# Evacuation priority, spread values, a third bank and the order of table functions in a hybrid decoder step

## The chip, the cores and the metric

The kernel runs on one core of one Trainium2 chip. Its time is the device time of one execution in microseconds. A core has five engines with a queue each: TensorE (matmuls and the loads of their stationary operand), VectorE, ScalarE, GpSimd and SyncE, which here issues the DMAs. Each queue is worked off in the order in which it was written. TensorE writes to PSUM, eight banks of 512 float32 values per partition, and VectorE or ScalarE must read ("evacuate") a bank before it can be used again; GpSimd has no part in that.

## The reference

One step of a one-layer decoder for a prompt of 512 tokens and 8 sample sequences of 4 tokens each, 544 columns in all, with a model width of 1024:

```python
h  = RMSNorm_pre(x)
P  = h @ w_in      # GLU value | gate | r | k | v | low-rank decay, iclr, gate | merge gates
A  = GLU -> causal depthwise conv (31) -> LayerNorm -> swish -> projection
# RWKV-7, per head of 64:
decay = exp(-exp(w_log));  a = sigmoid(iclr_base + l_iclr @ w_iclr_up)
kk = k * k_k;  kk = kk * rsqrt(max(sum(kk * kk), 1e-24))
s  = s * w_t - (s @ kk) (kk * a) + v k      # per token
y  = s @ r
B  = ((group_norm(y) + bonus) * g) -> projection
x  = x + RMSNorm_post((sigmoid(gA) * A + sigmoid(gB) * B) @ w_out)
x  = x + RMSNorm_post2(relu(RMSNorm_pre2(x) @ w_ff_up)^2 @ w_ff_down)
```

Outputs are both groups' tokens and the new states of the convolution, the token shift and the recurrence.

## The kernel before, in words

Channels lie on partitions and tokens on columns. A product with weights is made in three matmuls: each float32 operand is split into an upper and a lower part, and upper x upper, upper x lower and lower x upper are summed in one bank. `part_steps` (L145) writes such a product for one half of the columns (272 or 276 of them): 8 blocks of the contraction, 24 matmuls, then a call of `evac`, which is given by the caller and reads the bank. Weights arrive by DMA (`wraw`), are split by `wsplit` into an upper part (a cast on ScalarE or, for most blocks of `w_in`, on GpSimd, L140) and a lower part (VectorE, L141).

There are three stages. The first normalises the input (to about 50 us). The second (to about 780 us) works through eight pairs of heads and, between them, through the blocks of `w_in`, the gates and the convolution. The third makes the output projections and the feed-forward part and is nearly all linear products.

In the second stage one pair p has these parts. Blocks K, R and W (`block`, L799) are the linear products for k, r and v, with a token-shift evacuation on ScalarE and VectorE (L378 to L386). `rates` (L443) makes the decay and the iclr by two small products with sigmoid evacuations, a running sum of the decay (L460), exponentials of that sum with three different outputs (`pin`, `epp`, `eps`), and the norm of the keys: square, a sum over each head by a matmul (`sum_steps`, L439), a logarithm and an exponential. `front` builds the matrices of the eight chunks of 64 tokens and calls `inverse`, a triangular inverse on VectorE and by matmuls (L608). `value` makes the bonus term. `tokens` transposes. `chain` (L653) is the recurrence over the eight chunks: in each, matmuls into `ch`, a copy to `xs` on ScalarE (L667), a matmul (L671), a scaling on ScalarE (L673), a matmul (L675) and another scaling (L679), each waiting for the one before. `sample` (L692) does the 8 short sequences: it solves for `uv` (L745), spreads it over the sequences into `ux` by eight multiplications with columns of a mask on GpSimd (L754), and multiplies (L758) to update the states `st` (L760, L762). `groupnorm` (L766) follows a pair's recurrence; its last product is evacuated at L795.

The program is written in the order chain(p-1), K, rates, front, R, W, value, tokens, inverse, sample for pair p, then groupnorm(p-1), then `fill`: blocks of linear products for the gates and the convolution, which depend on no pair. This is not the order of the queues. A planner gives each instruction a priority by its place in the program, the earlier the higher, and builds the order of each queue from what is ready by its own cost estimates; `tc.high_priority(offset=n)` moves what is written in it ahead by n places (or back, where n is negative: the convolution runs at -300). The `yield` statements have no effect on that order where a generator is simply run to its end (`run`), or only mark where `until` stops. An engine takes its queue strictly in the planned order.

Three other things set the order. First, `tact` (L232) chains all activations that need a table set in the order of the program, and puts in a load of the set where it changes; `rates` goes through the sets for sigmoid, exponential, logarithm and exponential again, `groupnorm` needs one more. Second, tiles of one tag share the buffers of the tag in turn. Third, PSUM in the second stage: pool `pl` for linear products has 2 banks, `pb` takes 2, and the tags `ax`, `aux`, `yt` and `ch` have one bank each, 8 in all. `ax` serves the rates, all sums over heads, the bonus and the group norm; `aux` the sample part; `yt` and `ch` the recurrence (`ch` also the transposes).

Of the kernel before, what the change touches and what calls it, by code (L numbers as in the profile page):

```python
# [8 lines left out]
F32 = mybir.dt.float32  # L9
# [8 lines left out]
NB = 8  # L18
TS = 4
# [3 lines left out]
C = 64  # L23
# [5 lines left out]
CDEC = math.exp(-0.5)  # L29
NFP, NFIRST, NPG, UB = 44, 6, 2, 2  # L30
KEPT = 2
CP, HP, HN = 300, 900, 130
PUMP, WB, WL, WR = 5, 2, 2, 2
PE, ACT, DVE, SP, POOL = (getattr(mybir.EngineType, e) for e in ("PE", "Activation", "DVE", "SP", "Pool"))

# [27 lines left out]
def hybrid_step(ctx: ExitStack, tc: tile.TileContext, xT, hist, s0, win, wco, wro, wo, wup, wdn, lora,  # L63
# [12 lines left out]
    pg = ctx.enter_context(tc.tile_pool(name="pg", bufs=16))  # L76
    cv = ctx.enter_context(tc.tile_pool(name="cv", bufs=1))
    wp = ctx.enter_context(tc.tile_pool(name="wp", bufs=WB))
    pl = ctx.enter_context(tc.tile_pool(name="pl", bufs=2, space=PSUM))
    dr = ctx.enter_context(tc.tile_pool(name="dr", bufs=1, space=bass.MemoryType.DRAM))  # L80

    vt = cp.tile([128, NV], F32, name="vt")
# [31 lines left out]
    def con(name):  # L114
        o = COFF[name]
        return cs[:, o:o + dict(CONSTS)[name]]
# [28 lines left out]
    def part_steps(w, xs, s, o, m, evac, pool, tag):  # L145

        n = len(w)
        ps = pool.tile([128, 512], F32, name=tag, tag=tag)[:, 0:m]
        for k in range(n):
            (whi, wlo), (xhi, xlo) = w[k], xs[k]  # L150
            for i, (a, b) in enumerate(((whi, xhi), (whi, xlo), (wlo, xhi))):
                nc.tensor.matmul(ps, a, b[:, o:o + m], start=k == 0 and i == 0, stop=k == n - 1 and i == 2)  # L152
            if k == n - 1:
                evac(s, ps, o, m)
            yield

    def part_mm(*args):
# [74 lines left out]
    def tact(name, *args, **kw):  # L232

        with tables(name):
            lastact[0] = act(*args, **kw)
        return lastact[0]
# [42 lines left out]
    def sv(t):  # L279

        return t[:, T:N2].rearrange("p (b t) -> p b t", t=TS)
# [52 lines left out]
    with ExitStack() as c1:  # L334
# [101 lines left out]
        def sum_steps(lhsT, x, evac, pool, tag):  # L436
            for s, (o, m) in enumerate(S2):
                ps = pool.tile([128, 512], F32, name=tag, tag=tag)[:, 0:m]
                nc.tensor.matmul(ps, lhsT, x[:, o:o + m], start=True, stop=True)  # L439
                evac(s, ps, o, m)  # L440
                yield ACT

        def rates(p):  # L443

            lraw = page("k2")[:, 0:128]
            nc.sync.dma_start(lraw, lora[p, :, 0:128])
            yield (ACT,)
            glu_sig()
            yield
            for i in range(2):  # L450
                split_hl(up[0][H[i], i, :], up[1][H[i], i, :], lraw[H[i]])
            yield
            ap_ = p1.tile([128, 2 * N2], F32, name="ap", tag="ap")
            sg, a, pin = page("sg"), ap_[:, 0:N2], ap_[:, N2:2 * N2]
            for i, (d, b) in enumerate(((sg, "decay_base"), (a, "iclr_base"))):
                for s, (o, m) in enumerate(S2):
                    yield from part_steps([(up[0][:, i], up[1][:, i])], [ld], s, o, m,
                                          lambda s, ps, o, m: tact(SIG, d[:, o:o + m], ps, AF.Sigmoid, bias=vec(b, p)),
                                          qc, "ax")
            nc.vector.tensor_tensor_scan(sg[:, 0:N2], con("scan"), sg[:, 0:N2], 0.0, MULT, ADD)  # L460
            ep = p1.tile([128, NC * (C + 1) + 40], F32, name="ep")
            e0 = NC * (C + 1)
            epp = ep[:, 0:e0].rearrange("p (c t) -> p c t", c=NC)
            eps = ep[:, e0:e0 + 40].rearrange("p (b f) -> p b f", f=TS + 1)
            nc.vector.memset(epp[:, :, 0:1], 1.0)
            nc.vector.memset(eps[:, :, 0:1], 1.0)
            yield ACT
            tact(EXP, pin[:, 0:N2], sg[:, 0:N2], AF.Exp, scale=CDEC)
            yield (ACT,)
            tact(EXP, epp[:, :, 1:C + 1], ch3(sg), AF.Exp, scale=-CDEC)  # L470
            yield (ACT,)
            tact(EXP, eps[:, :, 1:TS + 1], sv(sg), AF.Exp, scale=-CDEC)
            yield ("K", p, ACT)

            k = pgs["k", p]
            k2 = page("k2")
            act(k2[:, 0:N2], k[:, 0:N2], AF.Square, scale=vec("k_k", p))
            yield
            rs = page("rs")
            yield from sum_steps(con("blk1"), k2, lambda s, ps, o, m: act(rs[:, o:o + m], ps, AF.Relu, bias=kk_neg), qc, "ax")  # L480
            tact(LN, rs[:, 0:N2], rs[:, 0:N2], AF.Ln, scale=2.0 ** 20, bias=kk_eps)
            yield (ACT,)
            kp = page("k2")
            act(kp[:, 0:N2], a[:, 0:N2], AF.Identity, scale=vec("k_a", p), bias=oka[:, p:p + 1])
            tact(EXP, rs[:, 0:N2], rs[:, 0:N2], AF.Exp, scale=-0.5, bias=kk_log)
            yield DVE
            st2(kp[:, 0:N2], k[:, 0:N2], kp[:, 0:N2], MULT)
            st2(a[:, 0:N2], a[:, 0:N2], pin[:, 0:N2], MULT)
            yield (DVE,)
            kk = page("kk")  # L490
            stt(out=kk[:, 0:N2], in0=k[:, 0:N2], scalar=vec("k_k", p), in1=rs[:, 0:N2], op0=MULT, op1=MULT)
            yield DVE
            pgs["pre"] = ep, epp, eps, a, pin, kk, kp
# [66 lines left out]
        def value(p):  # L560

            f, v, rk = fs[p], pgs["v", p], pgs["k", p]
            bon = f["bon"] = p2.tile([128, N2], F32, name="bon")
            yield from sum_steps(con("blk1"), rk, lambda s, ps, o, m: tt(out=bon[:, o:o + m], in0=ps,
                                                                       in1=v[:, 64 + o:64 + o + m], op=MULT),
                                 qc, "ax")
            if p:
                yield ("smp", p - 1, ACT)
            nc.scalar.copy(vpad[:, :, 32:64], v[:, 64 + T:64 + N2].unsqueeze(1).to_broadcast([128, 2, 32]))
            yield  # L570
# [121 lines left out]
        def sample(p):  # L692
# [55 lines left out]
            for i in range(2):  # L748
                tt(out=y[H[i], :], in0=xy[0:64, 320 + 32 * i:352 + 32 * i],
                   in1=xc[0:64, 64 * i + 32:64 * i + 64], op=ADD)  # L750
            for b in range(0, NB, 4):
                ux = p1.tile([128, 4, 64], F32, name="ux")
                for e in range(4):
                    nc.gpsimd.tensor_scalar(ux[:, e, :], uv[:, 0:64], con("bmask")[:, b + e:b + e + 1], None, MULT)  # L754
                yield
                if b == 0:
                    ps = qc.tile([128, NB, 64], F32, name="aux", tag="aux")
                nc.tensor.matmul(ps[:, b:b + 4].rearrange("p b v -> p (b v)"), zbt, ux.rearrange("p b v -> p (b v)"),  # L758
                                 start=True, stop=True)
            tt(out=st, in0=ps, in1=st, op=ADD)  # L760
            for b in range(NB):
                nc.gpsimd.tensor_scalar(st[:, b, :], st[:, b, :], f["epS"][:, b:b + 1], None, MULT)  # L762
# [3 lines left out]
        def groupnorm(p):  # L766
            f, y = fs[p], pgs["y", p]
            nc.scalar.copy(y[:, T:N2], ys[p])
            yc, sq = page("t0", cv), page("t1", cv)
            lraw = yc[:, 0:128]  # L770
            nc.sync.dma_start(lraw, lora[p, :, 128:256])
            lhi = p1.tile([128, 128], F32R, name="lhi")
            llo = p1.tile([128, 128], F32R, name="llo")
            yield ACT
            split_hl(lhi, llo, lraw)
            yield

            def cevac(s, ps, o, m):
                act(sq[:, o:o + m], ps, AF.Square)
                nc.scalar.copy(yc[:, o:o + m], ps)  # L780
            yield from sum_steps(con("cent"), y, cevac, qc, "ax")
            yield
            rs = sq
            yield from sum_steps(con("blkm"), sq,
                                 lambda s, ps, o, m: tact(LNEXP, rs[:, o:o + m], ps, AF.Ln, bias=gn_eps), qc, "ax")
            tact(LNEXP, rs[:, 0:N2], rs[:, 0:N2], AF.Exp, scale=-0.5)
            yield DVE
            o = yc[:, 0:N2]
            stt(out=o, in0=o, scalar=vec("lnx_g", p), in1=rs[:, 0:N2], op0=MULT, op1=MULT)
            yield DVE  # L790
            stt(out=o, in0=f["bon"], scalar=vec("lnx_b", p), in1=o, op0=ADD, op1=ADD)
            yield
            for s, (oo, m) in enumerate(S2):
                yield from part_steps([(lhi, llo)], [lg], s, oo, m,
                                      lambda s, ps, oo, m: tt(out=yc[:, oo:oo + m], in0=ps, in1=yc[:, oo:oo + m], op=MULT),  # L795
                                      qc, "ax")
            nc.sync.dma_start(o_dr[p], o)

        def block(b, p):  # L799
# [146 lines left out]
    for j in range(KT):  # L946
# [3 lines left out]
        def evac(s, ps, o, m):  # L950
            q = slice(o, o + m)
            tt(out=g[:, q], in0=ps, in1=g[:, q], op=MULT)
            tt(out=g[:, q], in0=g[:, q], in1=ms[j][:, q], op=ADD)
            split_hl(hl[0][:, q], hl[1][:, q], g[:, q])
# [192 lines left out]
```

## Time and profile before

| | |
|---|---|
| median of three runs | 1377.77 us (1374.94 to 1379.05) |
| the profiled execution | 1375.78 us, its span 1373.6 us |
| busy, whole span | TensorE 1266.3, VectorE 811.7, ScalarE 672.5, GpSimd 245.5 us |
| mean granted clock of TensorE | 0.963 |
| table loads on ScalarE | 45, 57.7 us |
| GpSimd at L754 (spread of the values) | 64 operations, 33.9 us |

The tables of the profile give busy time per engine and group, and for the idle time in front of an instruction the engine and line that released it. An idle engine costs something only where the end of the program waits for it. `PE` is TensorE, `PEld` its weight loads, `DVE` VectorE, `ACT` ScalarE, `POOL` GpSimd and `SP` SyncE. Matmuls overlap in the records, so that their durations add up to more than the time they take; busy time counts overlapping time once.

### The profile page before, as it was taken

The page shows a single profiled execution, that of the slowest core. Times are in us where ns is not written, and L with a number is a line of the kernel's source. Part 1 is how long each engine was busy: PE and PEld are TensorE (multiplying, and loading weights), DVE is VectorE, ACT ScalarE, POOL GpSimd, SP SyncE. Part 2 cuts the span into 40 slices and gives each one's busy share as a digit, 9 for nine tenths or more (in the row PEclk, how much of TensorE's full clock was granted, in tenths as well). Part 3 has the DMA queues.
Part 4 walks back from the last instruction along what each step waited for, and adds up shares of the span by engine and source line. Part 5 has one row for each costly group of instructions (what it writes and reads, how often), then busy time and mean ns, then how long its engine had stood idle before and what let it go on. Part 6 is the DMA issues. An engine that isn't in the chain of part 4 may idle for free.

```text
span 1373.6 us, 23314 instructions
## 1 busy us (share of the span) xinstructions
PE 1266.3 (92%) x9170; PEld 1192.4 (87%) x9170; DVE 811.7 (59%) x1521; ACT 672.5 (49%) x1595; POOL 245.5 (18%) x376
## 2 busy tenths in 40 slices
PE   6978998989899798898889999999999999999996
PEld 5968887787787778778788999999999999999995
DVE  5798768653876768767657746566833221333345
ACT  7452746657374563743733438245755322555231
POOL 2125333142433225232230120000000000000000
PEclk9999998999999899999999999999999999999998
DMA  5312111111201212012121565245023222322331
GB/s 183 99 46 90 45 47 48 30 65 34 77 18 42 77 34 64 31 42 87 33 65 44 177 215 173 89 128 177 28 62 93 86 84 83 101 81 91 93 93 66
DMA packets 46333, 110.61 MB, mean 81 GB/s; under 512 B 7184, under 2 KB 17680, under 8 KB 46224
## 3 DMA queue, kind: packets, MB, share of 16 engines
q1 hardware_dynamic: 46080, 109.05, 25.0%
q8 instruction: 72, 1.18, 0.3%
q14 instruction: 37, 0.30, 0.1%
q10 hardware_dynamic: 144, 0.07, 0.0%
HBM read 94.79 MB, written 14.32 MB: 79 GB/s over the span
## 4 chain that ended last, share of the span: by engine, by line
PE 64%; ACT 9%; DVE 7%; POOL 4%; issue 3%; DMA 1%; SPq 0%; DVEq 0%; POOLq 0%; ACTq 0%
PE lin L152 47%; PE pb L608 4%; ACT SV L679 2%; PE ax L439 2%; POOL ux L754 2%; POOL st L762 2%; PE ch L664 2%; PE ch L675 2%; ACT SV L673 2%; PE ch L671 1%; PE ax L152 1%; DVE c L292 1%; PE yt L668 1%; PE pb L544 1%; PE ch L666 1%
## 5 line engine op out<-in xcount | busy, mean ns | idle before, releaser
L152 PE MATMUL lin<-xh,whi 128*128 128x272 f32 (+1 forms) x2096 | 623.8, 298 | 22.1 <-DVE r L379 10.3
L152 PE MATMUL lin<-xh,wlo 128*128 128x272 f32 (+1 forms) x2096 | 624.5, 298 | 0.6 <-DVE wlo L141 0.6
L152 PE MATMUL lin<-xl,whi 128*128 128x272 f32 (+1 forms) x2096 | 622.4, 297 | 0.1
L152 PEld LDWEIGHTS lin<-xh,whi 128*128 128x128 f32 x2096 | 405.4, 194 | 25.7 <-issue 13.6
L152 PEld LDWEIGHTS lin<-xh,wlo 128*128 128x128 f32 x2096 | 405.0, 193 | 1.9 <-DVE wlo L141 0.8
L152 PEld LDWEIGHTS lin<-xl,whi 128*128 128x128 f32 x2096 | 404.6, 193 | 1.3 <-DVE xl L174 0.3
L141 DVE TENSOR_TENSOR wlo<-raw,whi 128x1024 fp32r<-128x1024 f32 x131 | 160.6, 1226 | 211.1 <-ACT whi L140 175.9
L292 DVE SCALAR_TENSOR_TENSOR c<-u,cw,c 128x512 f32<-128x512 f32 x240 | 187.0, 779 | 8.9 <-issue 4.8
L140 ACT CAST whi<-raw 128x1024 fp32r<-128x1024 f32 x76 | 79.7, 1049 | 122.4 <-PE lin L152 118.8
L140 POOL CAST whi<-raw 128x1024 fp32r<-128x1024 f32 x55 | 65.3, 1187 | 314.6 <-issue 166.0
L152 PE MATMUL lin<-xh,wl 128*128 128x272 f32 x240 | 69.4, 289 | 0.0
L152 PE MATMUL lin<-xl,wh 128*128 128x272 f32 x240 | 69.3, 289 | 0.0
L152 PE MATMUL lin<-xh,wh 128*128 128x272 f32 x240 | 69.2, 288 | 0.0
L1006 DVE TENSOR_TENSOR xl<-ff,xh 128x272 fp32r<-128x272 f32 x64 | 28.3, 442 | 55.9 <-ACT ff L1005 55.9
L228 ACT ACT_TABLE_LOAD x45 | 57.7, 1283 | 2.0 <-PEq L1129 1.2
L679 ACT ACTIVATE SV<-ch,pc 64x64 f32<-64x64 f32 x128 | 39.5, 309 | 20.4 <-PE ch L675 19.1
L673 ACT ACTIVATE SV<-ch 64x64 f32<-64x64 f32 x128 | 27.9, 218 | 37.0 <-PE ch L671 35.1
L152 PEld LDWEIGHTS lin<-xh,wh 128*128 128x128 f32 x240 | 45.2, 188 | 0.1
L152 PEld LDWEIGHTS lin<-xh,wl 128*128 128x128 f32 x240 | 45.2, 188 | 0.1
L152 PEld LDWEIGHTS lin<-xl,wh 128*128 128x128 f32 x240 | 45.1, 188 | 0.1
L754 POOL TENSOR_SCALAR ux<-uv,cs 128x64 f32<-128x64 f32 x64 | 33.9, 549 | 51.6 <-DVE uv L745 47.2
L762 POOL TENSOR_SCALAR st<-st,epS 128x64 f32<-128x64 f32 x64 | 40.0, 648 | 11.4 <-DVE rt L588 5.8
(275 smaller groups left out, 1894.1 us busy)
## 6 DMA issues: line engine op xcount, KB each, us to landing
raw<-win SPq DMA_DIRECT2D x58, 512.0 KB, 3.6
raw<-wup SPq DMA_DIRECT2D x32, 512.0 KB, 3.6
raw<-wdn SPq DMA_DIRECT2D x32, 512.0 KB, 3.6
g_dr<-g SPq DMA_DIRECT2D x16, 272.0 KB, 2.3
raw<-wro SPq DMA_DIRECT2D x8, 512.0 KB, 3.9
raw<-wco SPq DMA_DIRECT2D x8, 512.0 KB, 3.6
raw<-wo SPq DMA_DIRECT2D x8, 512.0 KB, 3.6
x<-xT SPq DMA_DIRECT2D x8, 276.0 KB, 5.0
```

Source lines behind the costliest of these rows:

```text
L140: upper(hi, r)
L141: tt(out=lo, in0=r, in1=hi.bitcast(F32), op=SUB)
L152: nc.tensor.matmul(ps, a, b[:, o:o + m], start=k == 0 and i == 0, stop=k == n - 1 and i == 2)
L228: lastact[0] = nc.scalar.preload_act_table_set(name)
L292: stt(out=c[:, 0:T], in0=u[:, t:t + T], scalar=w[:, t:t + 1], in1=c[:, 0:T], op0=MULT, op1=ADD)
L439: nc.tensor.matmul(ps, lhsT, x[:, o:o + m], start=True, stop=True)
L608: nc.tensor.matmul(ps[:, c, :], lhsT(c), rhs[:, c, :], start=True, stop=True)
L673: nc.scalar.mul(SV[H[i], c, i, :], ch[H[i], 2, B[i]], -1.0)
L679: nc.scalar.mul(SV[H[i], c + 1, i, :], ch[H[i], 1, B[i]], pc[H[i], c:c + 1])
L754: nc.gpsimd.tensor_scalar(ux[:, e, :], uv[:, 0:64], con("bmask")[:, b + e:b + e + 1], None, MULT)
L762: nc.gpsimd.tensor_scalar(st[:, b, :], st[:, b, :], f["epS"][:, b:b + 1], None, MULT)
L1006: tt(out=lo[:, q], in0=t[:, q], in1=hi[:, q].bitcast(F32), op=SUB)
```

## The change

It makes four edits.

The evacuation of every product that goes through `part_steps`, in all stages, gets a priority 300 places higher.

The values `uv` are spread over the sequences by one VectorE multiplication of 128 x 512 elements with both inputs broadcast, instead of eight GpSimd multiplications of 128 x 64 in two groups; one matmul of 512 columns takes the place of two of 256, and `ux` is twice as large.

The tag `ax` goes. The rates, the key sums and the bonus use `aux` (with the sample part), the group norm uses `yt` (with the recurrence). Pool `pl` gets the bank that this frees, three in place of two.

In `rates` the three exponentials of the running sum move behind the logarithm, next to the exponential that follows it.

```diff
-CP, HP, HN = 300, 900, 130
+CP, HP, HN, EV = 300, 900, 130, 300
...
-    pl = ctx.enter_context(tc.tile_pool(name="pl", bufs=2, space=PSUM))
+    pl = ctx.enter_context(tc.tile_pool(name="pl", bufs=3, space=PSUM))
...
             if k == n - 1:
-                evac(s, ps, o, m)
+                with tc.high_priority(offset=EV):
+                    evac(s, ps, o, m)
...
                     yield from part_steps([(up[0][:, i], up[1][:, i])], [ld], s, o, m,
                                           lambda s, ps, o, m: tact(SIG, d[:, o:o + m], ps, AF.Sigmoid, bias=vec(b, p)),
-                                          qc, "ax")
+                                          qc, "aux")
...
-            yield ACT
-            tact(EXP, pin[:, 0:N2], sg[:, 0:N2], AF.Exp, scale=CDEC)
-            yield (ACT,)
-            tact(EXP, epp[:, :, 1:C + 1], ch3(sg), AF.Exp, scale=-CDEC)
-            yield (ACT,)
-            tact(EXP, eps[:, :, 1:TS + 1], sv(sg), AF.Exp, scale=-CDEC)
-            yield ("K", p, ACT)
...
-            yield from sum_steps(con("blk1"), k2, lambda s, ps, o, m: act(rs[:, o:o + m], ps, AF.Relu, bias=kk_neg), qc, "ax")
+            yield from sum_steps(con("blk1"), k2, lambda s, ps, o, m: act(rs[:, o:o + m], ps, AF.Relu, bias=kk_neg), qc, "aux")
             tact(LN, rs[:, 0:N2], rs[:, 0:N2], AF.Ln, scale=2.0 ** 20, bias=kk_eps)
             yield (ACT,)
             kp = page("k2")
             act(kp[:, 0:N2], a[:, 0:N2], AF.Identity, scale=vec("k_a", p), bias=oka[:, p:p + 1])
             tact(EXP, rs[:, 0:N2], rs[:, 0:N2], AF.Exp, scale=-0.5, bias=kk_log)
+            tact(EXP, pin[:, 0:N2], sg[:, 0:N2], AF.Exp, scale=CDEC)
+            tact(EXP, epp[:, :, 1:C + 1], ch3(sg), AF.Exp, scale=-CDEC)
+            tact(EXP, eps[:, :, 1:TS + 1], sv(sg), AF.Exp, scale=-CDEC)
...
-            for b in range(0, NB, 4):
-                ux = p1.tile([128, 4, 64], F32, name="ux")
-                for e in range(4):
-                    nc.gpsimd.tensor_scalar(ux[:, e, :], uv[:, 0:64], con("bmask")[:, b + e:b + e + 1], None, MULT)
-                yield
-                if b == 0:
-                    ps = qc.tile([128, NB, 64], F32, name="aux", tag="aux")
-                nc.tensor.matmul(ps[:, b:b + 4].rearrange("p b v -> p (b v)"), zbt, ux.rearrange("p b v -> p (b v)"),
-                                 start=True, stop=True)
+            ux = p1.tile([128, NB, 64], F32, name="ux")
+            tt(out=ux, in0=uv[:, 0:64].unsqueeze(1).to_broadcast([128, NB, 64]),
+               in1=con("bmask").unsqueeze(2).to_broadcast([128, NB, 64]), op=MULT)
+            ps = qc.tile([128, NB, 64], F32, name="aux", tag="aux")
+            nc.tensor.matmul(ps.rearrange("p b v -> p (b v)"), zbt, ux.rearrange("p b v -> p (b v)"), start=True, stop=True)
             tt(out=st, in0=ps, in1=st, op=ADD)
```

In the same way the tag of the bonus sums in `value` becomes `aux`, and that of the two sums and the product in `groupnorm` becomes `yt`.

More of the change, by code (lines that the diff above doesn't have):

```diff
@@ L565, in value @@
                                                                        in1=v[:, 64 + o:64 + o + m], op=MULT),
-                                 qc, "ax")
+                                 qc, "aux")
             if p:
@@ L780, in cevac @@
                 nc.scalar.copy(yc[:, o:o + m], ps)
-            yield from sum_steps(con("cent"), y, cevac, qc, "ax")
+            yield from sum_steps(con("cent"), y, cevac, qc, "yt")
             yield
@@ L784, in groupnorm @@
             yield from sum_steps(con("blkm"), sq,
-                                 lambda s, ps, o, m: tact(LNEXP, rs[:, o:o + m], ps, AF.Ln, bias=gn_eps), qc, "ax")
+                                 lambda s, ps, o, m: tact(LNEXP, rs[:, o:o + m], ps, AF.Ln, bias=gn_eps), qc, "yt")
             tact(LNEXP, rs[:, 0:N2], rs[:, 0:N2], AF.Exp, scale=-0.5)
@@ L795, in groupnorm @@
                                       lambda s, ps, oo, m: tt(out=yc[:, oo:oo + m], in0=ps, in1=yc[:, oo:oo + m], op=MULT),
-                                      qc, "ax")
+                                      qc, "yt")
             nc.sync.dma_start(o_dr[p], o)
```

## The prediction

> **What bounds the kernel now.** I read the busy times by stage first, then what TensorE waited for in the stage that the change touches, then the granted clock around its longest waits, then single stretches of the timeline. The times of the runs shown are 1374.94 to 1379.05 us with a median of 1377.77 us; the profiled execution took 1375.78 us, 2.0 us under the median and 2.2 us over its own span. Differences are worked out on the profile and then taken off the median. About 0.3%, or 4 us, is what a measurement of this kernel can tell from no change.
>
> Busy time of each engine by stage (the columns are the stretch, its length, then busy time and count for each engine, the granted TensorE clock, the DMA share and GB/s):
>
> ```profile
> span 1373.6 us, 23314 instructions
> 0.00:50.00 50.00, 39.69 (x242) 35.72 (x243) 28.40 (x75) 29.83 (x79) 11.32 (x34) 0.97 0.49 162
> 50.00:780.00 730.00, 651.01 (x4383) 584.33 (x4382) 522.19 (x1010) 380.86 (x1020) 225.19 (x337) 0.94 0.18 57
> 780.00:1348.00 568.00, 563.11 (x4459) 560.73 (x4458) 244.66 (x397) 258.20 (x488) 9.00 (x5) 1.00 0.33 103
> 1348.00:1374.00 26.00, 12.53 (x93) 11.59 (x91) 16.42 (x41) 3.63 (x9) 0.00 (x0) 0.80 0.25 86
> ```
>
> From 780 to 1348 us TensorE has 4.9 us without work at full clock: nothing to win there. From 50 to 780 us, the stage of the eight head pairs, it is idle for 730 - 651 = 79 us and its clock is 0.94. No other engine is near its limit (VectorE 72%, ScalarE 52%). Its work there is fixed, and products with weights that depend on no pair are left to fill it until the end of the stage, so a microsecond of idle that is taken away ends the stage a microsecond earlier. This idle time by releaser (engine, line and what it waited for: us in total, times, longest):
>
> ```profile
> PE aux L758 <- POOL ux L754: 18.6, 14, 2.9
> PE lin L152 <- DVE r L379: 10.3, 4, 6.6
> PE pb L608 <- ACT nw L601: 9.6, 7, 4.0
> PE ch L675 <- ACT SV L673: 5.5, 13, 0.6
> PE ch L664 <- ACT SV L679: 3.8, 11, 0.7
> PE ch L671 <- ACT xs L667: 3.7, 3, 1.3
> PE lin L152 <- DVE rt L588: 3.2, 1, 3.2
> PE lin L152 <- DVE R L590: 2.7, 1, 2.7
> ```
>
> The first row is the spread of values by GpSimd. The rows of `lin` are linear products that could not begin, the largest behind an evacuation on VectorE that frees their bank. The rows of `ch` are the recurrence waiting for copies on ScalarE. Each idle stretch is paid twice, as the clock after it shows:
>
> ```profile
> 276.00:281.00 5.00, 2.30 (x14) 1.75 (x13) 2.94 (x7) 0.38 (x2) 4.53 (x8) 1.00 0.51 164
> 281.00:286.00 5.00, 5.00 (x29) 5.00 (x28) 2.76 (x13) 0.50 (x1) 3.54 (x8) 0.66 0.14 57
> 73.00:81.00 8.00, 3.99 (x19) 4.02 (x20) 8.00 (x13) 5.03 (x13) 4.92 (x7) 0.57 0.22 66
> 114.00:122.00 8.00, 6.80 (x30) 6.62 (x31) 6.20 (x16) 0.39 (x1) 6.11 (x9) 0.57 0.22 66
> 353.00:357.00 4.00, 3.48 (x14) 3.31 (x15) 1.67 (x5) 0.00 (x0) 3.09 (x8) 0.57 0.00 0
> 541.00:545.00 4.00, 3.57 (x17) 3.60 (x18) 4.00 (x12) 1.15 (x3) 0.53 (x1) 0.57 0.00 0
> 565.00:572.00 7.00, 6.14 (x28) 6.14 (x29) 6.93 (x14) 3.21 (x11) 5.84 (x8) 0.51 0.28 85
> 705.00:712.00 7.00, 6.08 (x26) 5.58 (x25) 3.29 (x15) 0.39 (x1) 4.63 (x11) 0.51 0.28 94
> ```
>
> After 2.7 us of idle between 276 and 281 us, which is a wait for the spread values, the next five microseconds run at 0.66. The work lost is busy time times (1 - clock): 1.7, 2.9, 1.5 and 3.0 us after spread waits (281, 114, 353, 705), together 9.1; and 1.7, 1.5 and 3.0 us after bank waits (73, 541, 565), together 6.2.
>
> **Part A, the spread on VectorE.** Per pair eight operations of GpSimd go, in two groups of four, and two matmuls; one operation of VectorE and one matmul of double width come.
>
> ```profile
> L754 POOL TENSOR_SCALAR ux<-uv,cs 128x64 f32<-128x64 f32 x64 | 33.9, 549 | 51.6 <-DVE uv L745 47.2 <-PE aux L758 2.8 <-ACT c L289 1.6
> L760 DVE TENSOR_TENSOR st<-aux,st 128x512 f32<-128x512 f32 x8 | 5.5, 692 | 17.4 <-PE aux L758 17.4
> L292 DVE SCALAR_TENSOR_TENSOR c<-u,cw,c 128x512 f32<-128x512 f32 x240 | 187.0, 779 | 8.9 <-issue 4.8
> 436.56 0.70 PE L758 MATMUL aux<-ux,zbt 128*128 128x256 f32 x2 [0.18 <-POOL ux L754]
> 439.20 0.70 PE L758 MATMUL aux<-ux,zbt 128*128 128x256 f32 x2 [1.46 <-POOL ux L754]
> ```
>
> Four operations at 549 ns are 2.2 us, and the second group cannot start before the first matmul has read the only buffer; that is the 1.46 us in the last row. The new operation is not in the trace; its nearest row is L760, the same size with two inputs, 692 ns. Left of the wait are between nothing and 8 x 0.69 = 5.5 us. I take half, 2.8, so 18.6 - 2.8 = 15.8 us are gained. Were the operation stuck each time behind one step of the convolution as well (779 ns, L292), 6.2 us on top of the 5.5 would be left: the gain is then 6.9. VectorE's 5.5 us more are hidden by its 28% of free time; 33.9 us leave GpSimd, whose queue stood 47.2 us at L754 waiting for `uv` with weight conversions behind it. The matmul streams the same columns: nothing. Of the 9.1 us of clock I take three quarters, 6.8, between 0 and 9.1.
>
> The page "TensorE: Matmul & The Clock Gate" of the Trainium skill (section "Why this matters for your kernels") says that only idle gaps over about 3 us between bursts bring the clock down. By it these waits, at most 2.9 us long, would cost no clock, and the sum below would be 23.9 us and the time 1354. The trace disagrees: 0.66 after 2.7 us.
>
> **Part B, third bank and raised evacuations.** Linear products wait 10.3 + 3.2 + 2.7 = 16.2 us in six waits. A third bank lets TensorE run one more group of 24 matmuls ahead, at 568 / 4459 = 0.127 us each 3.1 us. The longest wait, 6.6, leaves 3.5, the one of 3.2 leaves 0.1, the others nothing: 12.6 us gained, between 0 (the order of the queues is laid out anew, so the third bank can stay unused) and 16.2. Raising the evacuations works on the same waits and gets no term. Of the 6.2 us of clock I take half, 3.1, between 0 and 6.2, since the stretch at 565 has waits of the recurrence in it too. From 780 us on the raised evacuations meet a TensorE that does not wait; the 4.9 us of idle there bound a gain, and I put a loss at the same size; I take nothing.
>
> The bank comes from merging tags. `aux` now serves the rates, both sums and the sample part, `yt` the recurrence and the group norm. In the trace the recurrence of a new pair would meet the group norm of the old one:
>
> ```profile
> 437.09 0.38 PE L668 MATMUL yt<-LR,SV 128*128 128x128 f32 x2
> 437.46 0.43 DVE L795 TENSOR_TENSOR t<-ax,t 128x272 f32<-128x272 f32 x1
> 475.15 0.45 ACT L673 ACTIVATE SV<-ch 64x64 f32<-64x64 f32 x2 [0.80 <-PE ch L671]
> ```
>
> The first `yt` matmul would move behind 437.46 + 0.43, 0.8 us later; what needs it next is the scaling of `SV` at 475.15, 37 us on. The inverse, which lies between, is the cover; without it this costs 8 x 0.8 = 6.4 us. I take nothing.
>
> **Part C, the logarithm first.** Three exponentials move behind the logarithm, so the table set is loaded for exponentials once per pair and not twice.
>
> ```profile
> L228 ACT ACT_TABLE_LOAD x45 | 57.7, 1283 | 2.0 <-PEq L1129 1.2
> 230.67 1.28 ACT L228 ACT_TABLE_LOAD   x1
> 231.96 0.27 ACT L667 COPY xs<-ch 128x128 f32<-128x128 f32 x1
> ```
>
> Eight loads of 1283 ns are 10.3 us of ScalarE, which is not the bound. They count where a load stands ahead of a copy of the recurrence, as at 230.67 ahead of `xs`. The recurrence waits 5.5 + 3.8 + 3.7 = 13.0 us for such copies. Three loads per pair stand near its first steps and one of them goes: a third, 4.3 us, between 0 and 13.0. The moved exponentials come later to VectorE by their own time only, behind a multiplication that is due first: nothing.
>
> **The sum.** 15.8 + 6.8 + 12.6 + 3.1 + 4.3 = 42.6 us. All five queues are laid out anew, and the waits left in the list show that such an order and the chip disagree in places; some waits will come up elsewhere. I let a third come back (between none and all), which leaves 28.4 us: 1347 for an execution like the profiled one, 1349 on the median.
>
> **Rivals.** *The third bank brings nothing.* The same page of the Trainium skill (section "HAM oscillation — how this bites in real kernels") found that double-buffering the output banks gave no further gain once the waits were gone by other means. As a mechanism here: the bank waits are VectorE being late, and a further group only waits in its turn. For it: VectorE is busy for all 8.00 us at 73 us. Against it: it is busy for 72% of the stage, so it catches up. Terms B go: 42.6 - 15.7 = 26.9, two thirds of it 17.9, time 1360. Chance 0.20.
>
> *Slower: evacuations ahead of the recurrence.* ScalarE works in order. An evacuation that is put early stands there until its matmuls have run, with copies of the recurrence behind it.
>
> ```profile
> ACT g L330 <- PE lin L152: 35.5, 9, 9.3
> ACT gsg L411 <- PE lin L152: 31.1, 12, 3.6
> L411 ACT COPY gsg<-lin 128x272 f32<-128x272 f32 x16 | 6.2, 385 | 31.1 <-PE lin L152 31.1
> ```
>
> ScalarE does stand at evacuations (first two rows). The recurrence has 8 pairs x 8 chunks x 3 copies = 192 places; held by one evacuation of 385 ns at each they cost 74 us, and from 58% of the places on the 42.6 us are gone. At two thirds it is 49.3, 6.7 us slower: 1384. Against it: ScalarE is half idle, so an evacuation seldom competes. Chance 0.15.
>
> *The waits only move.* The reordering deals as many waits as it removes, about 1377. Chance 0.10, since the spread wait has a cause of its own that is gone.
>
> **How the numbers follow.** The forecast, 1349, has 0.55. Faster by over 0.3% is 0.55 + 0.20 = 0.75, within it 0.10, slower 0.15. The forecast's own range goes from 1335 (nothing comes back) to 1363 (two thirds do). With all bounds taken at once, 18.6 + 9.1 + 16.2 + 6.2 + 13.0 = 63 us, it would be 1315; I put the low end at 1320 and the high end at 1386, just past the slower rival.
>
> **What would show it.** Right: no wait for `ux` over 5.5 us in total on TensorE; `lin` waits under 8 us; 37 table loads; fewer stretches under 0.7 of the clock; the stage from 50 us on shorter by about 28 us and the stretch after it unchanged. Wrong: `ch` waits well over 13 us (the slower rival), `lin` waits of 16 us again (the bank), or as much idle as before under other names.

## The result and the profile after

The changed kernel takes 1335.08 us (median of 4 runs, 1330.27 to 1336.26) against 1376.36 us (median of 4 runs beside it, 1374.7 to 1379.05) for the kernel before: a ratio of 0.969, 95% interval 0.966 to 0.972, or 41 us faster. The forecast was 1349. The profiled execution took 1336.26 us with a span of 1334.3 us. One execution further below, of the kernel with the scaling on VectorE, ran at a mean granted clock of 0.554 and took 1951.90 us; it is left out of that kernel's median and ratio.

First the busy times by stage, in the same columns as before. The second boundary is put where 568 us of the third stage remain, as in the kernel before:

```profile
span 1334.3 us, 23218 instructions
0.00:50.00 50.00, 42.59 (x255) 37.87 (x256) 30.09 (x77) 30.10 (x80) 11.33 (x34) 0.97 0.50 162
50.00:740.00 690.00, 638.64 (x4364) 570.47 (x4363) 519.67 (x1017) 372.22 (x1012) 187.29 (x274) 0.96 0.19 61
740.00:1308.00 568.00, 563.12 (x4442) 560.45 (x4442) 242.54 (x396) 256.44 (x486) 6.38 (x4) 1.00 0.32 103
1308.00:1334.00 26.00, 13.21 (x98) 12.26 (x96) 16.50 (x42) 3.99 (x9) 0.00 (x0) 0.82 0.25 87
```

The whole gain lies between 50 us and the end of the second stage: 730 became 690 us, and the stretch of 568 us after it has the same 563 us of TensorE work. In the stage TensorE's idle time fell from 79 us to 690 - 639 = 51 us, and what the clock takes, busy time times (1 - clock), from 651 x 0.06 = 39 us to 639 x 0.04 = 26 us. With these rounded figures the two together give 41 us, and the stage became 40 us shorter.

What TensorE waited for in that stage, from the list of its waits (total, times, longest):

```profile
PE pb L605 <- ACT nw L598: 25.9, 7, 6.2
PE aux L152 <- ACT sg L236: 4.3, 1, 4.3
PE ch L672 <- ACT SV L670: 2.3, 8, 0.7
PE ch L661 <- ACT SV L676: 2.0, 7, 0.7
PE aux L752 <- DVE R L587: 0.7, 1, 0.7
PE ch L668 <- ACT xs L664: 0.6, 2, 0.4
```

The spread wait of 18.6 us is 0.7 us now (L752). The linear products, 16.2 us before, are not in the list of this stage at all. The recurrence (`ch`) went from 13.0 to 4.9 us. One row grew: the first matmuls of the inverse's products (`pb`, L608 before) wait 25.9 us for ScalarE where they waited 9.6. The wait of 4.3 us on `aux` is for a sigmoid of `rates`, whose products now stand on a merged tag; all waits of products on the merged tags come to 8.1 us, and those on `ax` came to 6.3. Groups of instructions for the operations that the change put in or took out:

```profile
L749 DVE TENSOR_TENSOR ux<-uv,cs 128x512 f32<-128x512 f32 x8 | 5.5, 684 | 0.4 <-DVE rt L585 0.4
L752 PE MATMUL aux<-ux,zbt 128*128 128x512 f32 x16 | 8.7, 625 | 0.8 <-DVE R L587 0.7
L229 ACT ACT_TABLE_LOAD x37 | 47.5, 1283 | 1.8 <-PEq L1122 1.2
```

The spread takes 684 ns on VectorE (692 were estimated), and 37 table loads remain.

The longest of these waits of `pb` is shown here with what stands ahead of it, in the timeline of one pair. The rows are of GpSimd, VectorE, ScalarE and TensorE in that order, each with its start, its duration and in brackets the idle time before it:

```profile
412.83 4.28 POOL L755 TENSOR_SCALAR st<-st,epS 128x64 f32<-128x64 f32 x6
419.50 0.15 POOL L712 MEMSET st<- 128x64 f32 x1 [2.39 <-DMA wkvs<-st]
419.61 1.04 POOL L140 CAST whi<-raw 128x1024 fp32r<-128x1024 f32 x1
```

```profile
417.73 0.17 DVE L585 TENSOR_TENSOR rt<-R,nw 128x24 f32<-128x24 f32 x1
420.68 1.23 DVE L141 TENSOR_TENSOR wlo<-raw,whi 128x1024 fp32r<-128x1024 f32 x1 [2.79 <-POOL whi L140]
421.82 0.18 DVE L587 TENSOR_TENSOR R<-R,rt 128x24 f32<-128x24 f32 x1
424.75 0.29 DVE L175 TENSOR_TENSOR llo<-t,lhi 128x128 fp32r<-128x128 f32 x1 [2.00 <-ACT lhi L174]
429.16 0.43 DVE L590 STREAM_TRANSPOSE td<-R 128x256 f32<-128x256 f32 x1
```

```profile
424.42 0.30 ACT L174 CAST lhi<-t 128x128 fp32r<-128x128 f32 x1 [6.83 <-DMA t<-lora]
429.68 0.40 ACT L598 COPY nw<-td 32x256 f32<-32x256 f32 x1 [3.88 <-DVE td L590]
```

```profile
431.46 3.65 PE L605 MATMUL pb<-nw,NQ 128*128 128x64 f32 x16 [6.20 <-ACT nw L598]
```

GpSimd scales the sample states, waits for their store with a memset, and only then converts weights. VectorE's subtraction for these weights waits 2.79 us for that, and behind it in VectorE's queue stand the steps of the inverse (L585, L587). A second wait of VectorE, 2.00 us, is for the gate's low-rank weights, which ScalarE can split only when their DMA has landed. The inverse ends at 429.6, ScalarE copies it, and TensorE has waited 6.2 us.

In this way VectorE stands for converted weights inside the inverse of six pairs of the changed kernel, 1.9 to 4.1 us each, 17 us in all. In three of the six the memset lies between the scaling and the conversion, as here; in the other three the conversion follows the scaling at once. In the pair whose `pb` matmuls start at 672 us there is no such wait, and TensorE waits 3.1 us all the same.

What follows is seen in the granted clock, here for two pairs:

```profile
430.00:438.00 8.00, 6.54 (x34) 6.57 (x34) 5.28 (x8) 4.67 (x11) 2.85 (x4) 0.57 0.21 66
672.00:680.00 8.00, 7.75 (x40) 7.78 (x40) 0.47 (x2) 1.27 (x3) 0.00 (x0) 0.57 0.17 66
```

Both stretches lie behind a wait of `pb` and run at 0.57. Windows of one microsecond show eight stretches of the stage at half clock. Six of them begin at the six waits of `pb` that last 3.1 to 6.2 us, and one at the wait of 4.3 us on `aux`.

### The profile page after: what moved, and what is told of

The parts are those of the page before. It is cut to its first block, busy times and chain, and to the rows that moved or that the text cites. A ratio compares the mean times of both kernels' runs of the same rounds, so it can differ in the third digit from the quotient of the medians.

```text
span 1334.3 us, 23218 instructions
## 1 busy us (share of the span) xinstructions
PE 1257.6 (94%) x9154; PEld 1181.1 (89%) x9154; DVE 808.8 (61%) x1529; ACT 662.7 (50%) x1587; POOL 205.0 (15%) x312
## 4 chain that ended last, share of the span: by engine, by line
PE 58%; DVE 15%; ACT 11%; issue 8%; DMA 5%; POOL 3%; SPq 1%; DVEq 0%; POOLq 0%; ACTq 0%
PE lin L152 41%; PE pb L605 5%; DVE c L293 2%; DVE wlo L141 2%; POOL st L755 2%; ACT SV L676 2%; ACT SV L670 1%; PE ch L672 1%; PE ch L661 1%; PE yt L440 1%; DVE rt L585 1%; PE pb L541 1%; PE aux L721 1%; DMA t<-lora 1%; DMA raw<-wo 1%
## 5 line engine op out<-in xcount | busy, mean ns | idle before, releaser
L152 PEld LDWEIGHTS lin<-xh,whi 128*128 128x128 f32 x2096 | 400.3, 191 | 6.1 <-DVE g L911 2.3
L152 PEld LDWEIGHTS lin<-xh,wlo 128*128 128x128 f32 x2096 | 400.6, 191 | 4.0 <-DVE wlo L141 1.8
L152 PEld LDWEIGHTS lin<-xl,whi 128*128 128x128 f32 x2096 | 399.9, 191 | 2.6 <-issue 1.2
L605 PE MATMUL pb<-nw,NQ 128*128 128x64 f32 x128 | 25.4, 381 | 25.9 <-ACT nw L598 25.9
L605 PEld LDWEIGHTS pb<-nw,NQ 128*128 128x128 f32 x128 | 24.3, 292 | 27.3 <-issue 27.3
L755 POOL TENSOR_SCALAR st<-st,epS 128x64 f32<-128x64 f32 x64 | 43.3, 699 | 12.7 <-DVE st L753 8.5
```

The lines of the kernel that those rows point to most:

```text
L605: nc.tensor.matmul(ps[:, c, :], lhsT(c), rhs[:, c, :], start=True, stop=True)
```

## The experiments

Three questions were open: which edit gave what; whether the third bank or the raised priority ended the bank waits; and what makes the inverse late. The table puts the times together. The ratio is to the kernel before on the same chip, with its 95% interval; the two last columns are TensorE's waits by name in the second stage of the profiled execution. As in the kernel before, where they were 16.2 and 13.0 us, `lin` counts the waits of linear products for VectorE and `ch` those of the recurrence for ScalarE.

| Kernel | Median us | Ratio | Wait of `pb` for ScalarE, us | Other waits, us |
|---|---|---|---|---|
| spread alone | 1357.32 | 0.988 (0.983 to 0.993) | 20.7 | `lin` 12.9, `ch` 12.0 |
| bank alone | 1348.99 | 0.980 (0.978 to 0.982) | 22.3 | spread 19.5, `lin` 4.3, `ch` 3.9 |
| priority alone | 1346.71 | 0.978 (0.974 to 0.981) | 8.4 | spread 17.0, `lin` 4.0, `ch` 3.7 |
| logarithm alone | 1372.60 | 0.997 (0.995 to 0.998) | 16.6 | spread 21.4, `lin` 10.8, `ch` 9.9 |
| changed, no priority | 1335.42 | 0.970 (0.965 to 0.974) | 30.9 | `lin` 0.3 |
| changed, no bank | 1334.08 | 0.970 (0.966 to 0.973) | 17.9 | `lin` 4.9 |
| changed, scaling on VectorE | 1304.01 | 0.947 (0.945 to 0.950) | | |
| the same again | 1300.43 | 0.946 (0.944 to 0.948) | 9.4 | `lin` for GpSimd 6.0, after the stage |
| changed, two state buffers | 1346.49 | 0.978 (0.973 to 0.982) | 26.2 | as the changed kernel |
| changed, kept state tile | 1328.67 | 0.965 (0.963 to 0.967) | 24.6 | |
| changed, again | 1338.20 | 0.972 (0.970 to 0.974) | 25.3 | as above |
| scaling, kept tile, own weights | 1306.40 | 0.951 (0.948 to 0.954) | 9.6 | `lin` for GpSimd 6.0, after the stage |

**Each edit by itself**, put into the kernel before; the edits are those of the diff above. The first is the spread:

> The kernel before with the spread on VectorE alone. If each edit removes its own waits: the 18.6 us of waits for the spread values fall under 5.5 us, 15 to 23 us faster than before, while the waits of linear products stay near 16 us and the wait of the inverse's matmuls for ScalarE near 10 us. If instead any edit mainly makes the planner lay the queues out anew: the spread waits go too, but the other two rows move by over 10 us in sum and the time lands anywhere within 10 us of before.

The time is 1.2% lower, 16 us by the ratio and 19 by the medians (the executions lie between 1352.6 and 1366.6), at the low end of what the first theory asks for. The waits of linear products for VectorE fall a little, from 16.2 to 12.9 us. But the inverse's wait doubles. These are TensorE's waits:

```profile
PE pb L608 <- ACT nw L601: 20.7, 7, 4.0
PE lin L152 <- DVE r L379: 7.9, 3, 6.6
PE ch L671 <- ACT xs L667: 4.7, 6, 1.4
PE aux L755 <- DVE R L590: 1.9, 2, 1.2
```

The spread wait fell from 18.6 to 1.9 us. The inverse's grew from 9.6 to 20.7. Both theories hold in part: the cause that is taken away is gone, and something else comes up.

> The kernel before with the tags merged and the third bank for linear products alone. If the third bank bridges the waits: the waits of linear products for evacuations fall from 16 us to under 5 us and the time by 10 to 16 us. If VectorE is simply late and a further group waits in its turn (the rival of the prediction): these waits stay over 10 us and the time is within 4 us of before. If the merged tags cost: waits on aux or yt banks of over 6 us and slower.

```profile
PE pb L608 <- ACT nw L601: 22.3, 8, 5.7
PE aux L758 <- POOL ux L754: 19.5, 15, 3.0
PE lin L152 <- DVE r L379: 4.3, 2, 3.5
PE ch L664 <- ACT SV L679: 2.6, 9, 0.5
```

The third bank bridges the waits: 16.2 became 4.3 us. The rival of the prediction, that it brings nothing, is wrong. The gain is 28 us and about twice what was asked for. The recurrence's waits fell from 13.0 to 3.9 us as well, which no theory had, and the stage's loss to the clock from 39 to 25 us. No product that moved to a merged tag waits longer than 1.0 us.

> The kernel before with the raised priority of evacuations alone. If late evacuations are what linear products wait for: their waits fall from 16 us to under 8 us and the time by 5 to 10 us. If raised evacuations hold up the recurrence on ScalarE: the waits of the recurrence rise from 13 us to over 20 us and the time rises. If priority seldom decides: under 4 us either way.

```profile
PE aux L759 <- POOL ux L755: 17.0, 11, 3.0
PE pb L609 <- ACT nw L602: 8.4, 7, 2.8
PE lin L152 <- DVE R L591: 2.7, 1, 2.7
PE ch L665 <- ACT SV L680: 2.3, 8, 0.6
PE ch L676 <- ACT SV L674: 1.4, 6, 0.4
```

Raised priority alone takes away the same waits and is worth 30 us. The recurrence waits 3.7 us for ScalarE and not over 20: the slower rival, evacuations ahead of the recurrence, does not happen. Two smaller waits for GpSimd came up, 4.1 us for `BK` and 3.8 us for `zbk`.

> The kernel before with the logarithm ahead of the exponentials alone: 37 table loads in place of 45. If the loads matter where they stand ahead of a copy of the recurrence: the waits of the recurrence fall from 13 us to about 9 us and the time by about 4 us. If ScalarE's time does not count at all: under 2 us. If the planner's new order is what counts: over 5 us either way, in waits of other names.

The gain is 4 us, as forecast, and the waits of the recurrence went from 13.0 to 9.9. Other rows moved too (spread 21.4, inverse 16.6), so that the agreement of the total is not proof of the way.

The inverse's wait rose with the spread, the bank and the logarithm, each alone; only with the raised priority alone did it stay at 8 us.

**One edit undone.** The four gains by themselves add up to 19 + 28 + 30 + 4 = 81 us; together they gave 41. Which two overlap:

> The changed kernel without the raised priority of evacuations. If the third bank and the raised priority take away the same waits (alone they gave 28 and 30 us, the whole change 41): at most 8 us slower than the changed kernel, 1335 to 1343, with linear products waiting under 6 us. If they add: about 20 us slower, 1355, with these waits back over 10 us.

> The changed kernel with the old tags and two banks. If bank and priority take away the same waits: at most 8 us slower than the changed kernel, 1335 to 1343. If they add: about 20 us slower, 1355, with linear products waiting over 10 us. If the merged tags or the third bank are what lets the inverse run late: its wait falls from 26 us to about the 8 us that it has with the raised priority alone.

TensorE's waits without the priority, and then without the bank:

```profile
PE pb L604 <- ACT nw L597: 30.9, 8, 6.2
```

```profile
PE pb L605 <- ACT nw L598: 17.9, 8, 4.3
PE lin L152 <- DVE R L587: 4.0, 2, 2.5
```

Both kernels stay at the time of the changed kernel, 1335 and 1334 us, and linear products wait 0.3 and 4.9 us for VectorE. The third bank and the raised priority take away the same waits; either would have done, as far as intervals of 5 to 6 us to each side can tell. With the larger of the two counted once, 53 of the 81 us are left, and the 12 us from there to 41 are not assigned to an edit; the inverse's wait grew with several of the edits. It is 17.9 us without the third bank and 30.9 without the priority; neither falls to the 8 us of the priority alone, so the bank alone is not what makes the inverse late.

**Why the inverse is late.** The scaling of the states (L755, eight operations on GpSimd) moves to VectorE:

```diff
-            for b in range(NB):
-                nc.gpsimd.tensor_scalar(st[:, b, :], st[:, b, :], f["epS"][:, b:b + 1], None, MULT)
+            tt(out=st, in0=st, in1=f["epS"].unsqueeze(2).to_broadcast([128, NB, 64]), op=MULT)
```

> The changed kernel with the scaling of the sample states by one VectorE multiplication in place of eight on GpSimd. If the inverse's matmuls wait because GpSimd is late (scaling, then a memset that waits for the store, then a weight conversion that VectorE's subtraction and so the inverse stand behind): the wait of 26 us falls under 15 us and the time by 8 to 16 us, to 1319 to 1327. If the inverse is late only because steps of the convolution lie between its own on VectorE: the wait stays over 20 us and the time within 4 us of the changed kernel.

The kernel takes 1304 us, 30 us less than the changed kernel by the two ratios. A second measurement has the profile:

> The scaling of the sample states on VectorE, once more, for a profile of an undisturbed execution: about 1305 us. If GpSimd's lateness made the inverse late, as its 30 us suggest: the inverse's wait is under 10 us where the changed kernel has 26, and the clock lost after it goes with it. If the gain came from the planner's new order alone: the wait of the inverse is still over 15 us and other rows have shrunk.

It takes 1300 us, 38 us less than the changed kernel on the same chip (1338, below). Its waits on TensorE, of which that for `whi` comes after the stage, at 718 us:

```profile
PE pb L605 <- ACT nw L598: 9.4, 8, 2.0
PE lin L152 <- POOL whi L140: 6.0, 1, 6.0
PE ch L661 <- ACT SV L676: 1.6, 7, 0.3
```

Its busy times in the stage:

```profile
50.00:704.00 654.00, 623.73 (x4378) 557.45 (x4377) 522.18 (x1023) 372.85 (x1014) 144.38 (x210) 0.98 0.20 65
```

The inverse's wait is under 10 us. TensorE is idle for 654 - 624 = 30 us of the stage (51 in the changed kernel) and loses 624 x 0.02 = 12 us to the clock (26). VectorE's wait for converted weights, in the same list of the kernel before, of the changed kernel and of this one:

```profile
DVE wlo L141 <- POOL whi L140: 27.8, 12, 3.8
```

```profile
DVE wlo L141 <- POOL whi L140: 39.2, 15, 4.5
```

```profile
DVE wlo L141 <- POOL whi L140: 15.0, 10, 3.4
```

Inside the inverse this wait is gone from every pair. From the first of its thirty steps on VectorE to its transposition (L590) the inverse takes 163 us over the eight pairs, against 186 in the changed kernel. Steps of the convolution still stand between its own, so they are not the main cause of the long waits. What is not separated is the planner's new order, which every edit brings.

The first row also says what this experiment does not explain. In the kernel before, VectorE waited for converted weights as well, 16 us of it inside the inverse against 17 in the changed kernel, behind the same scaling (L762 there); and the inverse took 192 us, no less than the 186 now. Still `pb` waited 3 us or more in two pairs only, and in six now. The inverse did not become slower; TensorE comes to its products sooner, relative to it. With the scaling off GpSimd the inverse is shorter, but that does not show why the four edits made TensorE wait for it.

Two smaller parts of the same chain were tried. The first is two buffers for the states (`p2.tile` in place of `p1.tile` for `sx`):

> The changed kernel with two buffers for the sample states, so that the memset of the next pair does not wait for the store of the last. If that wait (11 us on GpSimd, seven times) is what makes the weight conversion and then the inverse late: the inverse's wait of 26 us falls by 8 us or more and the time by 5 to 12 us. If the scaling itself, 5.5 us a pair, is what counts: under 4 us. If steps of the convolution are: nothing.

This took no wait away. With a second buffer the memset of the pair after next is planned into the same place and waits for the store as before (10.1 us against 11.4); the inverse waits 26.2 us. A tile kept over all pairs removes the memset itself:

```diff
+        sx = p1.tile([128, NB + 1, 64], F32, name="st")
+        nc.gpsimd.memset(sx[:, NB, :], 0.0)
...
-            sx = p1.tile([128, NB + 1, 64], F32, name="st")
-            nc.gpsimd.memset(sx[:, NB, :], 0.0)
```

> The changed kernel with one tile for the sample states that is kept over all pairs, its zero column set once: the memset of each pair, which waits 1 to 2.5 us for a store, is gone from GpSimd's queue, the scaling stays there. If that memset's wait ahead of the weight conversion makes the inverse late: the inverse's wait of 26 us falls under 15 us and the time by 8 to 16 us. If the eight scalings, 5.5 us a pair, are what makes GpSimd late: a fall of the wait by 2 us a pair at most, and the time within 6 us of the changed kernel.

The wait stays at 24.6 us, so the memset is not what makes the inverse late. Of the chain on GpSimd that leaves the scaling, with the planner's order as the part that is not separated. The time, 9.5 us under the changed kernel on the same chip, lies in the range of the first theory, but without the fall of the wait that it asks for, and no single row explains it.

**The scatter.** Two buffers left TensorE's queue word for word as in the changed kernel, and its idle time; still the time was 11 us longer, on another chip.

> The changed kernel itself, to see how far its time scatters. Two buffers for the sample states left the order and the waits on TensorE as they were (77.3 us of idle against 76.5) and yet measured 11 us more, in the clock. If the length of the slow stretches after an idle stretch is left to chance in each execution: this kernel gives times between 1330 and 1350 too. If it belongs to the program: it stays within 1330 to 1337.

The changed kernel stays between 1335.7 and 1340.2 us here (1330.3 to 1336.3 in the first measurement), the one with two buffers between 1340.1 and 1352.6. That fits neither theory: the changed kernel leaves the 1330 to 1337 of the second and does not reach the 1350 of the first. The stage in the profiles of the changed kernel, run again, and of the one with two buffers, whose stage goes on for some 7 us behind this window:

```profile
50.00:740.00 690.00, 640.15 (x4360) 572.29 (x4358) 518.36 (x1015) 371.63 (x1011) 187.02 (x274) 0.96 0.19 60
```

```profile
50.00:740.00 690.00, 639.20 (x4302) 571.96 (x4301) 511.07 (x1005) 370.88 (x1009) 184.94 (x272) 0.94 0.18 57
```

Idle time is 50 and 51 us; the clock is 0.96 and 0.94, and the spans, 1334.8 and 1341.8 us, differ by 7 us. But two executions of one program differ in the same way. Here are two windows in the first profile of the changed kernel and then the same windows in the second, with the same order on TensorE:

```profile
600.00:601.00 1.00, 1.00 (x7) 1.00 (x6) 0.00 (x0) 0.00 (x0) 0.00 (x0) 0.50 0.00 0
684.00:685.00 1.00, 1.00 (x10) 0.94 (x10) 0.02 (x1) 0.00 (x0) 0.00 (x0) 1.00 0.00 0
```

```profile
600.00:601.00 1.00, 1.00 (x12) 1.00 (x11) 1.00 (x2) 0.00 (x0) 0.00 (x0) 1.00 0.00 0
684.00:685.00 1.00, 1.00 (x6) 1.00 (x6) 0.00 (x0) 0.00 (x0) 0.00 (x0) 0.50 0.00 0
```

Behind the wait of `pb` at 592 us the first execution is still at half clock at 600 us and the second is not; behind that at 672 us (668 in the second) it is the other way round. So how long the clock stays down after the same wait differs from one execution to the next. Whether the program with two buffers is slower in itself is left open: it was measured four times and on another chip, its ratio (0.973 to 0.982) touches that of the changed kernel (0.970 to 0.974), and the changed kernel without the priority scatters by as much alone (1329.3 to 1342.4).

**All of it together.** Scaling on VectorE, the kept tile, and the gate's low-rank weights loaded early into a tile of their own:

```diff
+            lq = pgs["lq", p] = p2.tile([128, 128], F32, name="lq")
+            nc.sync.dma_start(lq, lora[p, :, 128:256])
...
-            lraw = yc[:, 0:128]
-            nc.sync.dma_start(lraw, lora[p, :, 128:256])
+            lraw = pgs["lq", p]
```

> The changed kernel with the scaling on VectorE, the kept tile without the memset, and the gate's low-rank weights loaded into a tile of their own with the pair's other low-rank weights, so that ScalarE does not stand 3 to 7 us a pair waiting for them. If what stands ahead of the inverse is what remains: 1290 to 1305, below the scaling on VectorE alone. If the inverse is no longer late with the scaling moved: 1300 to 1310, no gain over it.

It takes 1306 us: no gain over the scaling alone (1300 us), and the inverse waits 9.6 us in it too. The best version of this study is the changed kernel with the scaling on VectorE, 5.4% (5.2 to 5.6) under the kernel before.

## Why the prediction was right, and where it was off

**The bound** was read rightly: the gain is idle time and clock of TensorE in the stage of the pairs, and the third stage did not move.

**Part A** held. Of 18.6 us 0.7 remain, 2.8 were forecast. By itself the edit gave 16 us (the ratio of 0.988), between the 22.6 of its two terms and two thirds of them, 15.

**Part B** had the right mechanism, and the size was too small. 12.6 of the 16.2 us were to go; all went. The step that said raising the evacuations "works on the same waits and gets no term" held: undoing either costs nothing that the runs can tell. What the part left out is the recurrence: its waits fell by 9 us with the bank alone and with the priority alone, where only part C was given any of that. Linear products that can start may fill the places between its steps; that is argued and not shown. The merged tags, taken at nothing, cost 1.8 us of waits.

**Part C** held in its total, 4.3 us forecast and 4 measured alone, and that is partly luck: the recurrence's waits fell by 3.1 us, the inverse's grew by 7.0, and the rest came from other rows and the clock.

**The give-back** was the guess of the sum, a third or 14.2 us, under no name. The waits that the three parts name gave 42.2 us of idle time (17.9, 16.2 and 8.1) where 32.7 were forecast. A third of these 32.7 is 10.9 us; what came back is 16.3 us, and it is one wait: `pb`, from 9.6 to 25.9 us. That a third was near the truth is luck, as no row stood behind it. The prediction quoted the row of `pb` and never asked what it waits for. What stands ahead of it could be seen in the trace before: GpSimd's row for L762 (64 operations, 40.0 us) stands beside the one that the change moved. Why the wait grew stays open.

**The clock** was where the forecast fell short together with B: 9.9 us in its two terms, 6.6 after the give-back, and 13 measured. The terms came from stretches behind spread and bank waits, 15.3 of the 39 us that the stage lost. Slow stretches among the steps of the recurrence stood in no term, as at 236 and 662 us of the kernel before, where no wait near is over 1.3 us:

```profile
236.00:237.00 1.00, 1.00 (x6) 1.00 (x6) 1.00 (x4) 0.86 (x2) 0.92 (x3) 0.50 0.78 319
662.00:663.00 1.00, 0.71 (x4) 0.66 (x4) 0.97 (x3) 0.96 (x6) 1.00 (x1) 0.50 0.43 49
```

Windows of one microsecond show fifteen slow stretches in the stage before and eight in the changed kernel, and none of the eight lies behind a wait of the recurrence for ScalarE.

**The forecast as a whole.** 28 us were forecast and 41 came, near the 42.6 that the sum had before its give-back. Half of the difference is idle time (28 us where 21.8 were left of 32.7), half is the clock. Of the signs that were named, the waits for `ux`, those of `lin`, the 37 table loads, the fewer slow stretches and the unchanged third stage came true; the stage became shorter by 40 us and not by 28.

**The rivals.** That the third bank brings nothing fell with the bank alone. That evacuations hold up the recurrence fell with the priority alone. That the waits only move was wrong as a whole: 42.2 us of the named waits went and 16.3 came up in `pb`.

The Trainium skill's page "TensorE: Matmul & The Clock Gate" (section "Why this matters for your kernels") asks for no idle gaps over about 3 us between bursts of matmuls. The trace of the kernel before does not agree with a limit there: the stretch at 281 us follows waits of 2.5 and 0.2 us (the 2.7 us of the prediction), and that at 353 us one of 1.3 us. The trace of the changed kernel comes near it: seven of its eight slow stretches begin at a wait of 3.1 to 6.2 us, and the eighth, at 79 us, follows waits of 1.4 and 1.9 us.

## What to carry to other kernels

Where TensorE is the bound and its queue is planned ahead, an idle microsecond costs more than itself, because the clock after it pays too, though not at one price: here 79 us of idle came with 39 us of clock, 51 with 26 in the changed kernel, 51 with 38 in the one with two buffers and 33 with 6 in the last of the table. Before giving a share of a gain back under no name, ask of each remaining wait what stands ahead of its releaser, engine by engine; here a queue of small GpSimd operations stood ahead of a conversion, a subtraction and the inverse, and moving it to VectorE gave another 30 to 38 us. Two edits that end the same wait are worth one, so measure each with the other undone.

## What the runs showed of the hardware that was not expected

In the changed kernel eight GpSimd multiplications of 128 x 64 elements take 5.4 us a pair (43.3 us for 64). With the scaling on VectorE, one multiplication of the same 128 x 512 elements with a broadcast input takes 686 ns.

The granted clock after an idle stretch is not a fixed price: behind the same wait in two executions of one program, with the same order on TensorE, one was at 0.50 of full speed at 684 us and the other at 1.00.
